# A hybrid decoder step: mixer steps placed later among the projection's products, bank copies put first

## The chip, the core and the metric

The program runs on one core of a Trainium2 chip. The metric is the device time of one launch in microseconds (us): 3565.34 us is the median of three runs before the change (3554.55 to 3570.49). A difference of 0.5%, some 18 us, is about what a measurement can tell from no change.

## The reference, cut to what matters

A trunk of two layers is run on 1024 prompt tokens and on 8 sequences of 4 new tokens each (1056 columns in all). One layer is:

```
proj = x @ w_in                                   # 46 chunks of 128 output rows
SSD : conv + SiLU, 16 heads, chunked scan, gated RMSNorm (2 groups of 8 heads)
MLA : latent queries/keys, causal attention on the prompt, paged cache for the new tokens
GDN : conv + SiLU, 4 heads, chunked delta rule (a triangular solve per chunk), gated RMSNorm
x = LayerNorm(alpha * x + [SSD | MLA | GDN] @ w_out)
```

Everything is float32. The projection's products are done as three products of rounded halves (`mm3`), the mixers' as plain float32 products.

## The kernel before, in words

Each layer has a phase one (projection and mixers) and a phase two (attention, decode over the paged cache, output projection). In phase one, `merge` (lines 422 to 444) writes TensorE's order by hand. It has two streams and a filler. Stream a runs the small per-token terms (`misc`), GDN heads 0 and 2, the latents' norm (`mla_in`) and SSD group 0. Stream b runs the input norm, GDN heads 1 and 3, the new tokens' GDN (`gdn_sample`) and SSD group 1. The filler is the projection (PSUM tiles `ps_pj`), then the latent products `mla_q` (`ps_pj<-cq`), the absorbed queries (`absorb`) and keys and values (`mla_kv`).

A stream is a generator. Where its next product needs a result of another engine it yields a number: its next step may not be placed before the planner's clock has advanced by so much. The clock counts columns of the products placed so far (`mm`, line 177: columns / 2400, times four for plain float32). While no stream is due, `merge` places filler products; when the filler is at its end or waits for something, the clock jumps to the next stream's time. So a yield does not wait: it fixes how many products stand between a step and the next one. TensorE runs them in this order and stands still where a result is late. The yield is the number that the change raises in four places:

```
        yield 2.98            # rstd, line 319: between the sums and the broadcast of 1/sqrt
        yield 5.2             # gdn_block, line 845: before the transposes of the normed output
        yield 2.03            # ssd_sample, line 1196: before each of 8 state products
```

Only TensorE's order is fixed in this way. VectorE (DVE), ScalarE (ACT), GpSimd (POOL) and SyncE's DMA queue (SP) get theirs from a scheduler that takes the program's order, readiness by its own estimate, and a priority; `high_priority()` lets what stands in it go ahead of other work that is ready. Each of these runs its queue in the order in which it was written.

Stream a's products write tiles `ps_a`, stream b's `ps_b`; each has three PSUM banks. A bank is free when the instruction that reads it out has run: a DVE or ACT copy or a DVE operation. Stream a works in `regA` (shown as `c`) and the tile `q`, stream b in `p1_b` (shown as `p_b`), their small tiles are `p_sa` and `p_sb`.

At the end of phase one these regions change hands. `absorb` writes its queries into `regA`; the attention's first query tiles are loaded into `q` (`q<-qd`, 14 DMAs); the decode's first page tiles `dec_v` lie where `p_b` and its neighbours were. The decode begins with products `ps_dS`.

Of the kernel before, what the change touches and what calls it, by code (L numbers as in the profile page):

```python
# [17 lines left out]
ALU = mybir.AluOpType  # L18
# [23 lines left out]
C_ID, C_ONES, C_BD, C_LV, C_INC, C_STR = 0, 128, 256, 384, 640, 768  # L42
C_M1, C_I1, C_L1 = 896, 928, 960
C_SUM = C_L1 + 128
C_INCS, C_STRS = C_SUM + 32, C_SUM + 64
# [82 lines left out]
class Builder:  # L128
# [48 lines left out]
    def mm(self, out, lhsT, rhs, start, stop):  # L177

        self.clock += out.free_size() * (1 if rhs.dtype in (F32R, BF16) else 4) / 2400 / {32: 4, 64: 2}.get(out.partition_size(), 1)
        return self.nc.tensor.matmul(out, lhsT=lhsT, rhs=rhs, start=start, stop=stop)  # L180
# [125 lines left out]
    def rstd(self, T, tag, ss, n, mul, eps, soon=contextlib.nullcontext):  # L306

        nc = self.nc
        ws = [(j, c, min(128, n - c)) for j, c in enumerate(range(0, n, 128))]
        ps, r = self.psum(tag), T(8)  # L310
        for j, c, w in ws:
            self.mm(ps[:w, j:j + 1], lhsT=ss[:, c:c + w], rhs=self.ones[:, 0:1], start=True, stop=True)
        full = n // 128
        with soon():
            for p, u in ((128, slice(0, full)), (n % 128, slice(full, full + 1))):
                if p:
                    nc.vector.tensor_scalar(out=r[:p, u], in0=ps[:p, u], scalar1=mul, scalar2=eps, op0=ALU.mult, op1=ALU.add)  # L317
                    nc.gpsimd.tensor_tensor(out=r[:p, u], in0=r[:p, u], in1=self.mhalf[:p, 0:1].to_broadcast([p, u.stop - u.start]), op=ALU.pow)  # L318
        yield 2.98
        ps = self.psum(tag)  # L320
        for j, c, w in ws:
            self.mm(ps[:, c:c + w], lhsT=r[:w, j:j + 1].to_broadcast([w, 128]), rhs=self.ident[:w, :w], start=True, stop=True)
        return ps[:, :n]
# [376 lines left out]
    def gdn_block(self, r, L, T, Q, h, nb, x, S, ahead):  # L700
        nc = self.nc
        k, q, v, zs, g, bt = x
        c0, _, nch = HALVES[nb]
        n = nch * 128
        cc = c0 // 128
# [7 lines left out]
        def tps(src):  # L713
            ps = self.psum(r)
            for w in ws:
                self.tp(ps[:, w], src[:, w])
            return ps[:, :n]

        def mms(lhs, rhs):
            ps = self.psum(r)  # L720
            for w in ws:
                mm(ps[:, w], lhsT=lhs[:, w], rhs=rhs[:, w], start=True, stop=True)
            return ps[:, :n]
# [7 lines left out]
        p, p2 = tps(k), tps(q)  # L731
# [8 lines left out]
        p = tps(v)  # L740
        self.tt(nc.vector, v3(vb), v3(p), bc(self.t_be[:, cc:cc + nch, h]))
        yield 3.9
        p = tps(kn)
# [4 lines left out]
        p = tps(qn)  # L748
# [13 lines left out]
        p, p2 = mms(kT, kb), mms(kT, qT)  # L762

        m = nch * 32
        Ac, Uc, Tc, Xc = (Q(m) for _ in range(4))
        c3 = lambda a: a.rearrange("p (c n) -> p c n", n=32)
        mk1 = lambda o: self.const[:, o:o + 32].unsqueeze(1).to_broadcast([128, nch, 32])
# [9 lines left out]
        def mmc(lhs, rhs):  # L777
            ps = self.psum(r)
            for c in range(nch):
                for u in gs:  # L780
                    w = slice(c * 32, c * 32 + 32)
                    mm(ps[u, w], lhsT=lhs[u, w], rhs=rhs[u, w], start=True, stop=True)
            return ps[:, :m]
# [3 lines left out]
        ahead()  # L787
        for lv in range(4):
            p = mmc(Ac, Tc)
            self.tt(nc.vector, c3(Xc), c3(p), mk1(C_L1 + 32 * lv))  # L790
            yield 1.3
            p = mmc(Uc, Xc)
            self.tt(nc.vector, Tc, Tc, p, ALU.subtract)
            nc.vector.transpose(Uc, Tc)
            yield 1.25
        v4 = lambda a: a.rearrange("p (c g n) -> p c g n", c=nch, g=4)
        for a, b, eng in ((Ti, Tc, nc.vector), (U, Uc, nc.gpsimd)):
# [3 lines left out]
        for lv in range(2):  # L801
            p = mms(at, Ti)
            self.tt(nc.vector, v3(X), v3(p), mk(C_LV + 128 * lv))
            yield 1.96
            if lv == 0:
                p = mms(U, X)
                self.tt(nc.vector, Ti, Ti, p, ALU.subtract)
                yield 1.65
                p = tps(Ti)
                nc.scalar.copy(out=U, in_=p)  # L810
            else:
                p = mms(X, U)
# [4 lines left out]
        p = mms(kbe, U)  # L817
# [4 lines left out]
        for c, w in enumerate(ws):  # L822
            p = self.psum(r)
            mm(p[:, :128], lhsT=U[:, w], rhs=vb[:, w], start=True, stop=S is None)
            if S is not None:
                mm(p[:, :128], lhsT=wT[:, w], rhs=S, start=False, stop=True)
                mm(po[:, w], lhsT=qe[:, w], rhs=S, start=True, stop=False)
            vn = Q(128)
            nc.vector.tensor_copy(out=vn, in_=p[:, :128])
            yield 1.42  # L830
            p = self.psum(r)
            mm(p[:, :128], lhsT=kd[:, w], rhs=vn, start=True, stop=True)
            mm(po[:, w], lhsT=attn[:, w], rhs=vn, start=S is None, stop=True)
            Sn = Q(128)
            if S is None:
                nc.vector.tensor_copy(out=Sn, in_=p[:, :128])
            else:
                e = (16 + h) * 16 + cc + c
                self.stt(Sn, S, self.elast[:, e:e + 1], p[:, :128], ALU.mult, ALU.add)
            S = Sn  # L840
            yield 1.3
        ro = norm(po, 1.0 / 128, RMS_EPS)
        on = t(T)
        self.tt(nc.vector, v3(on), v3(po), bc(ro))
        yield 5.2
        p = tps(on)
        self.stt(on, p, self.gnwh[:, 0:1], zs)
        self.mix_out(12 + h, c0, n, on)
# [157 lines left out]
    def ssd(self, r, g):  # L1006
        nc, l = self.nc, self.l
        R = Ring(self.reg[r][0])
        yield {-1, 17 + g * 10, 18 + g * 10}
        CT, Bt, CB, acc = R(NT), R(9 * 128), R(8 * 128 + 32), R(NT)  # L1010
        X, X2 = R.rest(), Ring(self.reg[r][1])
        BT = X(NT)
        self.dma(BT, self.pd[:, 16 + g * 2])
        self.dma(CT, self.pd[:, 17 + g * 2])
        yield 13.0
        for t0 in (0, 4, 8):
            p, p2 = self.psum(r), self.psum(r)
            for t in range(t0, min(t0 + 4, 9)):
                w = 128 if t < 8 else 32
                o = (t - t0) * 128  # L1020
                self.tp(p[:w, o:o + 128], BT[:, t * 128:t * 128 + w])
                self.mm(p2[:w, o:o + w], lhsT=BT[:, t * 128:t * 128 + w], rhs=CT[:, t * 128:t * 128 + w], start=True, stop=True)
            if t0 < 8:
                nc.scalar.copy(out=Bt[:, t0 * 128:t0 * 128 + 512], in_=p)  # L1024
                self.tt(nc.vector, CB[:, t0 * 128:t0 * 128 + 512].rearrange("p (c n) -> p c n", c=4), p2.rearrange("p (c n) -> p c n", c=4),
                        self.const[:, C_INC:C_INC + 128].unsqueeze(1).to_broadcast([128, 4, 128]))
            else:
                nc.scalar.copy(out=Bt[:32, 1024:1152], in_=p[:32, :128])
                self.tt(nc.vector, CB[:32, 1024:1056], p2[:32, :32], self.const[:32, C_INCS:C_INCS + 32])

        big = self.sm(r, F32R)
        K = slice(0, 96)
        bs = X(128)
        self.stack(bs.bitcast(F32R), Bt[0:32, 1024:1152], 1)
        self.tt(nc.gpsimd, big[K, 512:1536].rearrange("p (b n) -> p b n", b=8), bs[K].unsqueeze(1).to_broadcast([96, 8, 128]),
                self.const[K, C_BMT:C_BMT + 8].unsqueeze(2).to_broadcast([96, 8, 128]))
        for k in range(4):
            yield {19 + g * 10 + 2 * k, 20 + g * 10 + 2 * k}
            Y = Ring(X.a, X.base, X.size)
            yield from self.ssd_pair(r, Ring(Y(3 * 512)), Ring(X2.a), Ring(Y(6 * 128)), g * 4 + k, CT, Bt, CB, acc, k == 0)  # L1040
        yield from self.ssd_sample(r, X, X2, g, CT, Bt, CB, acc, big)
# [95 lines left out]
    def ssd_sample(self, r, X, T, g, CT, Bt, CB, acc, big):  # L1137
        nc, l = self.nc, self.l
# [19 lines left out]
        c3 = cm.rearrange("p (b t) -> p b t", b=8)  # L1158
# [4 lines left out]
        def old(bs):  # L1163
            for b in bs:
                q = (b % 4) * 32
                self.mm(py[q:q + 32, :], lhsT=c3[:, b], rhs=hb[b], start=b < 4, stop=b >= 4)
                el = self.elast.rearrange("p (h c) -> p h c", c=16)[:, h8, 8 + b]
                self.tt(nc.gpsimd, h3(hb[b]), h3(hb[b]), el.unsqueeze(2).to_broadcast([128, 8, 64]))
# [8 lines left out]
        p = self.psum(r)  # L1177
# [15 lines left out]
        for b in range(8):  # L1193
            if b == 4:
                old((6, 7))
            yield 2.03
            p = self.psum(r)
            self.mm(p, lhsT=b3[K, b], rhs=xs[K], start=True, stop=True)
            self.tt(nc.vector, hb[b], hb[b], p, ALU.add)
            self.dma(self.o["ssd_s"][l, :, g, b], hb[b])  # L1200
        self.tt(nc.vector, ys.rearrange("p (h n) -> p h n", n=64), py.rearrange("p (h n) -> p h n", n=64), ea.unsqueeze(2).to_broadcast([128, 8, 64]))
        yield 1.42
        p = self.psum(r)
# [779 lines left out]
```

## Time and profile before

| what | us |
|---|---|
| median of three runs | 3565.34 |
| lowest, highest | 3554.55, 3570.49 |
| profiled execution, its own time | 3572.76 |
| its span, first to last instruction | 3571.0 |
| layer 0: the attention's first score product starts at | 1060.45 |
| layer 0: the decode's first product starts at | 1075.21 |

The profile is of one execution. A row of the timeline has the start, the duration, the engine, the line, the operation, the tiles (written<-read), the shape and the count; in brackets stands how long the engine had been idle and what ended that. Plain float32 products appear twice each. Clock 1.00 is TensorE's level of 2.4 GHz, 0.50 that of 1.2 GHz; a stretch's number is the mean.

### The profile page before, as it was taken

What the parts mean: (1) busy time and instruction counts of PE and PEld (TensorE: products, weight loads), DVE (VectorE), ACT (ScalarE), POOL (GpSimd) and SP (SyncE); (2) the same over time, 40 slices, a digit from 0 to 9 for tenths busy, and PEclk for the clock granted to TensorE, in tenths of its full rate; (3) what the DMA queues carried; (4) which work ended last, traced back from release to release, by engine and by line L of the source; (5) the groups of instructions that cost most, each with busy time, mean ns of one, the idle gap of its engine ahead of it and who ended that gap; (6) DMA issues with size and microseconds to landing.
All of it is one profiled execution on the core that took longest, in us unless ns stands there. A gap on an engine that the chain in (4) does not pass through costs nothing. (4 is left out here: it accounts for less than half of the span.)

```text
span 3571.0 us, 82553 instructions
## 1 busy us (share of the span) xinstructions
PE 3124.5 (87%) x33880; PEld 2666.9 (75%) x33880; DVE 2234.9 (63%) x4646; ACT 1337.2 (37%) x3099; POOL 1124.5 (31%) x1214
## 2 busy tenths in 40 slices
PE   6889999888778988979979999898987788889797
PEld 5888988888665655559878899887886566556697
DVE  7766365687545766745586653657865466666455
ACT  5433234333133344434434332343322343434344
POOL 4434344644421211101134444355453111211000
PEclk7999999999888999989989999999998799999898
DMA  3322324555776655444424232255567755553453
GB/s 137 123 90 88 106 67 161 168 169 177 249 251 201 207 178 191 171 154 157 151 83 126 83 94 90 68 171 184 173 214 254 230 191 190 183 196 128 161 180 127
DMA packets 317070, 564.70 MB, mean 158 GB/s; under 512 B 51772, under 2 KB 218748, under 8 KB 299668
## 3 DMA queue, kind: packets, MB, share of 16 engines
q1 hardware_dynamic: 293140, 408.42, 35.9%
q0 software_dynamic: 23552, 151.01, 12.0%
q8 instruction: 266, 4.36, 0.5%
q14 instruction: 112, 0.92, 0.1%
HBM read 429.00 MB, written 130.30 MB: 157 GB/s over the span
## 5 line engine op out<-in xcount | busy, mean ns | idle before, releaser
L180 PE MATMUL ps_pj<-xh,w_r 128*128 128x384 f32 (+1 forms) x4416 | 1212.7, 342 | 50.8 <-ACT p_cv L471 17.2
L180 PEld LDWEIGHTS ps_pj<-xh,w_r 128*128 128x128 f32 x4416 | 816.1, 196 | 71.0 <-ACT p_cv L471 19.1
L180 PE MATMUL ps_pj<-xl,w_r 128*128 128x384 f32 (+1 forms) x2208 | 733.9, 332 | 4.6 <-POOL xl L153 4.0
L180 PEld LDWEIGHTS ps_pj<-xl,w_r 128*128 128x128 f32 x2208 | 432.4, 196 | 13.5 <-POOL xl L153 11.1
L180 PE MATMUL ps_m<-mix,wo 128*128 128x384 f32 (+1 forms) x2304 | 395.4, 333 | 44.1 <-DVE wo L153 19.3
L180 PEld LDWEIGHTS ps_m<-mix,wo 128*128 128x128 f32 x2304 | 385.4, 196 | 50.8 <-DVE wo L153 22.4
L156 DVE SCALAR_TENSOR_TENSOR p_cv<-p_cv,c 128x384 f32<-128x384 f32 (+1 forms) x432 | 335.0, 779 | 71.9 <-ACT p_cv L159 65.9
L180 PE MATMUL ps_dS<-dec_k,c 32*32 32x256 f32 x8192 | 314.7, 385 | 31.5 <-issue 12.8
L153 POOL TENSOR_TENSOR w_r<-w_raw,w_r 128x1024 fp32r<-128x1024 f32 (+1 forms) x98 | 233.2, 2379 | 293.5 <-ACT w_r L165 251.3
L180 PEld LDWEIGHTS ps_dS<-dec_k,c 32*32 32x32 f32 x8192 | 190.1, 106 | 135.7 <-issue 85.0
L1667 DVE STREAM_TRANSPOSE dec_k<-dec_v 128x2048 f32<-128x2048 f32 x128 | 290.9, 2282 | 0.1
L1643 POOL DMA_INDIRECT dec<-cache_k_rope,c x64 | 60.9, 951 | 566.0 <-DVE dec L1736 516.9
L153 DVE TENSOR_TENSOR wo<-c,wo 128x1024 fp32r<-128x1024 f32 x96 | 119.0, 1243 | 128.2 <-PE ps_m L180 98.3
L159 ACT ACTIVATE p_cv<-p_cv 128x384 f32<-128x384 f32 x144 | 72.8, 505 | 314.8 <-DVE p_cv L156 313.8
L1470 ACT COPY c<-ps_aT 128x512 f32<-128x512 f32 (+3 forms) x192 | 89.9, 478 | 248.0 <-PE ps_aT L150 241.2
L165 ACT CAST wo<-c 128x1024 fp32r<-128x1024 f32 x96 | 100.4, 1050 | 218.3 <-DMA c<-w_out 174.9
L1643 POOL DMA_INDIRECT dec_v<-cache_kv_latent,c x128 | 120.8, 943 | 182.9 <-PE ps_dV L180 157.6
L180 PE MATMUL ps_b<-p_b 128*128 128x128 f32 (+7 forms) x1476 | 156.8, 284 | 21.1 <-ACT p_b L1024 8.4
L1513 DVE TENSOR_REDUCE c<-ps_aS 128x1 f32<-128x512 f32 (+3 forms) x192 | 105.4, 549 | 101.7 <-PE ps_aS L180 96.3
L159 ACT ACTIVATE c<-ps_aS,c 128x512 f32<-128x512 f32 (+3 forms) x192 | 110.6, 576 | 153.7 <-DVE c L1514 138.6
L318 POOL TENSOR_TENSOR c<-c,c 128x3 f32<-128x3 f32 (+2 forms) x22 | 17.1, 783 | 472.6 <-DVE c L317 472.6
L180 PEld LDWEIGHTS ps_b<-p_b 128*128 128x128 f32 (+5 forms) x1476 | 133.6, 161 | 37.7 <-ACT p_b L1024 9.9
(325 smaller groups left out, 5601.6 us busy)
## 6 DMA issues: line engine op xcount, KB each, us to landing
c<-w_out SPq DMA_DIRECT2D x96, 512.0 KB
w_raw<-w_in SPq DMA_DIRECT2D x92, 512.0 KB
pd<-p_cv SPq DMA_DIRECT2D x164, 192.0 KB
p_b<-pd SPq DMA_DIRECT2D x66, 256.0 KB
c<-pd SPq DMA_DIRECT2D x64, 256.0 KB
q<-rowd SPq DMA_DIRECT2D x48, 256.0 KB
p_b<-rowd SPq DMA_DIRECT2D x48, 256.0 KB
pd<-p_cv SPq DMA_DIRECT2D x82, 144.0 KB
```

The costliest lines, as they stand in the source:

```text
L153: eng.tensor_tensor(out=out, in0=a, in1=b, op=op)
L156: self.nc.vector.scalar_tensor_tensor(out=out, in0=a, scalar=s, in1=b, op0=op0, op1=op1)
L159: self.nc.scalar.activation(out=out, in_=in_, func=func, **kw)
L165: self.nc.scalar.copy(out=hi, in_=src)
L180: return self.nc.tensor.matmul(out, lhsT=lhsT, rhs=rhs, start=start, stop=stop)
L318: nc.gpsimd.tensor_tensor(out=r[:p, u], in0=r[:p, u], in1=self.mhalf[:p, 0:1].to_broadcast([p, u.stop - u.start]), op=ALU.pow)
L1470: nc.scalar.copy(out=t[:, :w], in_=p[:, :w])
L1513: nc.vector.reduce_max(out=m, in_=ps[:, :w], axis=AX.X)
L1643: nc.gpsimd.indirect_dma_start(out=out, out_offset=None, in_=src, in_offset=bass.IndirectOffsetOnAxis(ap=idx[:, c:c + 1], axis=0))
L1667: nc.vector.transpose(T[r].rearrange("p j s k -> p j (s k)"), V[:, :, r * 128:r * 128 + 128])
```

## The change

Four yields are raised or added, all in phase one, and the instructions that read a mixer's bank out are put under `high_priority()` at three places.

```diff
@@ rstd
-        yield 2.98
+        yield 5.5
@@ gdn_block, the four levels of the 32-row solve, and the scan over chunks
             p = mmc(Ac, Tc)
-            self.tt(nc.vector, c3(Xc), c3(p), mk1(C_L1 + 32 * lv))
+            with self.tc.high_priority():
+                self.tt(nc.vector, c3(Xc), c3(p), mk1(C_L1 + 32 * lv))
             yield 1.3
             p = mmc(Uc, Xc)
-            self.tt(nc.vector, Tc, Tc, p, ALU.subtract)
-            nc.vector.transpose(Uc, Tc)
+            with self.tc.high_priority():
+                self.tt(nc.vector, Tc, Tc, p, ALU.subtract)
+                nc.vector.transpose(Uc, Tc)
...
-            nc.vector.tensor_copy(out=vn, in_=p[:, :128])
+            with self.tc.high_priority():
+                nc.vector.tensor_copy(out=vn, in_=p[:, :128])
...
-            if S is None:
-                nc.vector.tensor_copy(out=Sn, in_=p[:, :128])
-            else: ...
+            with self.tc.high_priority():
+                if S is None:
+                    nc.vector.tensor_copy(out=Sn, in_=p[:, :128])
+                else: ...
@@ gdn_block, before the transposes of the normed output
-        yield 5.2
+        yield 7.5
@@ ssd, the start of a group
         for t0 in (0, 4, 8):
+            if t0:
+                yield 2.5
             p, p2 = self.psum(r), self.psum(r)
...
-            if t0 < 8:
-                nc.scalar.copy(out=Bt[:, t0 * 128:t0 * 128 + 512], in_=p)
-                self.tt(nc.vector, CB[...], p2..., ...)
-            else: ...
+            with self.tc.high_priority():
+                if t0 < 8:
+                    nc.scalar.copy(out=Bt[:, t0 * 128:t0 * 128 + 512], in_=p)
+                    self.tt(nc.vector, CB[...], p2..., ...)
+                else: ...
@@ ssd_sample
         for b in range(8):
-            yield 2.03
+            yield 2.03 if b else 7.0
```

What this does to the order of the instructions is seen at three places of layer 0 (layer 1 is alike).

TensorE at the start of SSD group 0 (stream a). `ps_a<-c_58,c_144` is a transpose of the B rows, `ps_a<-c_144` the product of B with C. Before, the second set of four follows the first at once:

```order
L150 MATMUL ps_a<-c_58,c_144 128x128
L180 MATMUL ps_a<-c_144 128x128
L150 MATMUL ps_a<-c_58,c_144 128x128
L180 MATMUL ps_a<-c_144 128x128
L150 MATMUL ps_a<-c_58,c_144 128x128
L180 MATMUL ps_a<-c_144 128x128
L150 MATMUL ps_a<-c_58,c_144 128x128
L180 MATMUL ps_a<-c_144 128x128
```

After, from the last pair of the first set to the first pair of the second:

```order
L180 MATMUL ps_b<-p_sb 128x512
L180 MATMUL ps_pj<-xh,w_r 128x384
L180 MATMUL ps_pj<-xl,w_r 128x384
L180 MATMUL ps_pj<-xh,w_r 128x384 x2
L180 MATMUL ps_pj<-xl,w_r 128x384
L180 MATMUL ps_pj<-xh,w_r 128x384 x2
L180 MATMUL ps_pj<-xl,w_r 128x384
L180 MATMUL ps_pj<-xh,w_r 128x384
L150 MATMUL ps_a<-c_58,c_144 128x128
L180 MATMUL ps_a<-c_144 128x128
```

Fifteen products of the projection (six of them ahead of the first row shown) and one of stream b now stand between the two sets.

SyncE's DMA queue at the end of phase one. `c_144<-qd` are the loads of `absorb` (c_144 is `regA`), `q<-qd` those of the attention's first queries. Before, the last of the 14 query loads and what follows:

```order
L136 DMA q<-qd_161 64x4x128
L136 DMA q<-qd_162 64x2x128
L136 DMA q<-qd_161 32x4x128 x2
L136 DMA q<-qd_162 32x4x128
L136 DMA c_144<-w_ukT 64x2048
L136 DMA c_144<-qd_161 64x8x32
L136 DMA c_144<-qd_161 32x8x32
L136 DMA c_144<-qd_162 64x8x32
L136 DMA c_144<-qd_162 32x8x32
L136 DMA mixd<-p_b 128x288 x4
```

After, the loads of `absorb` come right behind the last stores of the queries, and the 14 loads stand further down:

```order
L136 DMA qd_161<-stage 128x384
L136 DMA qd_162<-stage 128x384
L136 DMA kr<-krx 64x1024
L136 DMA kr<-krx 32x1024
L136 DMA c_144<-w_ukT 64x2048
L136 DMA c_144<-qd_161 64x8x32
L136 DMA c_144<-qd_161 32x8x32
L136 DMA c_144<-qd_162 64x8x32
L136 DMA c_144<-qd_162 32x8x32
L136 DMA p_b<-ssd_st 128x512 x2
L136 DMA yd<-q 128x4x32
```

The 14 loads now stand behind stream a's last load into the tile `q` and its last stores from it.

TensorE at the change from phase one to phase two. `w_r,ck` are the value products of `mla_kv`, `ps_aS` the attention's scores. Before:

```order
L180 MATMUL ps_pj<-w_r,ck 128x512 x6
L180 MATMUL ps_a<-w_r,ck 128x512 x6
L180 MATMUL ps_aS<-kT,q 128x256 x2
L180 MATMUL ps_aS<-kr,q 128x256
L180 LDWEIGHTS c_124
L180 MATMUL ps_aS<-c_124 128x128
```

After, to the first three of the six small products of the norm that stand just before the same scores:

```order
L180 MATMUL ps_a<-w_r,ck 128x512 x6
L180 MATMUL ps_b<-p_sb 128x512 x2
L180 MATMUL ps_b<-c_58,p_b 128x32
L180 MATMUL ps_b<-p_b 64x32 x2
L180 MATMUL ps_b<-c_58,p_b 128x32
L180 MATMUL ps_b<-p_b 64x32 x2
L180 MATMUL ps_b<-c_58,p_b 128x32
L180 MATMUL ps_b<-p_b 64x32 x2
L180 MATMUL ps_b<-c_58,p_b 128x32
L180 MATMUL ps_b<-p_b 64x32 x2
L180 MATMUL ps_b<-c_58,p_b 128x1 x2
L180 MATMUL ps_b<-c_58,p_b 32x1
```

The last steps of stream b, the end of the new tokens' SSD and its norm, now stand behind the filler's last product, with nothing between them.

## Rows read from the trace of the kernel before

**Rows 1.** Busy time by stretch: PE, PEld, DVE, ACT, POOL; PEclk; DMA share, GB/s.
```profile
100.00:960.00 860.00, 779.82 (x7145) 731.27 (x7144) 551.44 (x1154) 297.90 (x728) 395.33 (x432) 0.96 0.43 137
```
**Rows 2.** Waits of PE, 60 to 1070 us: total, times, longest.
```profile
PE ps_pj L180 <- ACT p_cv L471: 9.3, 3, 3.8
PE ps_a L180 <- ACT c L1024: 9.2, 1, 9.2
...
PE ps_a L180 <- DVE p_sa L153: 7.4, 5, 4.8
...
PE ps_b L180 <- DVE p_sb L153: 5.2, 6, 2.1
PE ps_pj L180 <- DVE stage L153: 4.9, 4, 1.5
...
PE ps_a L180 <- DVE p_sa L829: 4.3, 3, 3.3
PE ps_b L180 <- ACT p_b L1024: 4.2, 1, 4.2
PE ps_a L180 <- DVE p_sa L836: 4.0, 1, 4.0
...
PE ps_a L180 <- POOL c L318: 2.4, 1, 2.4
```
**Rows 3.** Waits of PE in layer 1, 1830 to 2860 us.
```profile
PE ps_a L180 <- ACT c L1024: 9.5, 1, 9.5
PE ps_a L180 <- DVE c L153: 9.5, 1, 9.5
```
**Rows 4.** Timeline of all engines at the start of SSD group 0.
```profile
665.09 6.47 DVE L1092 TENSOR_SCALAR q<-q,c 128x128 f32<-128x128 f32 x7 [4.16 <-DMA q<-rowd]
...
673.57 0.79 PE L180 MATMUL ps_a<-c 128*128 128x128 f32 x2 [9.17 <-ACT c L1024]
```
**Rows 5.** Timeline of PE at the first state product of stream a.
```profile
920.48 0.42 PE L180 MATMUL ps_pj<-xh,w_r 128*128 128x384 f32 x1
...
922.49 0.34 PE L180 MATMUL ps_pj<-xh,w_r 128*128 128x384 f32 x1
927.62 0.77 PE L180 MATMUL ps_a<-p_sa 96*128 96x512 f32 x1 [4.79 <-DVE p_sa L153]
```
**Rows 6.** Busy time by stretch, around that wait and around the wait of `absorb`.
```profile
922.00:933.00 11.00, 6.21 (x23) 5.78 (x22) 7.07 (x14) 3.61 (x6) 4.24 (x4) 0.69 0.59 204
1031.00:1053.00 22.00, 13.14 (x48) 11.81 (x49) 4.88 (x9) 3.56 (x7) 2.55 (x3) 0.61 0.71 207
```
**Rows 7.** Timeline of PE, end of phase one.
```profile
1013.85 0.30 PE L180 MATMUL ps_b<-c,p_b 128*128 128x32 f32 x2
...
1024.23 0.94 PE L180 MATMUL ps_b<-c,p_b 128*128 128x128 f32 x6
...
1039.86 7.00 PE L180 MATMUL ps_a<-c 64*128 64x32 f32 x32 [8.93 <-DVE c L153]
...
1060.45 0.40 PE L180 MATMUL ps_aS<-kT,q 128*128 128x256 f32 x2
...
1075.21 1.10 PE L180 MATMUL ps_dS<-dec,c 32*32 32x256 f32 x16 [1.21 <-DVE dec L1722]
```
**Rows 8.** Timeline of SyncE's DMA queue, end of phase one.
```profile
1020.32 0.45 SPq L136 DMA_DIRECT2D yd<-p_b  x1
...
1024.09 0.38 SPq L136 DMA_DIRECT2D p_b<-yd  x1
...
1025.06 8.34 SPq L136 DMA_DIRECT2D q<-qd  x14
...
1036.69 2.01 SPq L136 DMA_DIRECT2D mixd<-p_b  x4
```
**Rows 9.** Timeline of POOL: the decode's first page load.
```profile
1041.69 1.22 POOL L1643 DMA_INDIRECT dec_v<-cache_kv_latent,c  x1 [1.42 <-DMA c<-gated]
```
**Rows 10.** Timeline of DVE in the first GDN blocks.
```profile
219.81 0.69 DVE L153 TENSOR_TENSOR p_b<-ps_b,p_sb 128x512 f32<-128x512 f32 x1 [2.18 <-POOL p_sb L674]
```

More of the change, by code (lines that the diff above doesn't have):

```diff
@@ L834, in gdn_block @@
             Sn = Q(128)
-            if S is None:
-                nc.vector.tensor_copy(out=Sn, in_=p[:, :128])
-            else:
-                e = (16 + h) * 16 + cc + c
-                self.stt(Sn, S, self.elast[:, e:e + 1], p[:, :128], ALU.mult, ALU.add)
+            with self.tc.high_priority():
+                if S is None:
+                    nc.vector.tensor_copy(out=Sn, in_=p[:, :128])
+                else:
+                    e = (16 + h) * 16 + cc + c
+                    self.stt(Sn, S, self.elast[:, e:e + 1], p[:, :128], ALU.mult, ALU.add)
             S = Sn
@@ L1022, in ssd @@
                 self.mm(p2[:w, o:o + w], lhsT=BT[:, t * 128:t * 128 + w], rhs=CT[:, t * 128:t * 128 + w], start=True, stop=True)
-            if t0 < 8:
-                nc.scalar.copy(out=Bt[:, t0 * 128:t0 * 128 + 512], in_=p)
[L1025 to L1029, printed above, removed]
+            with self.tc.high_priority():
+                if t0 < 8:
+                    nc.scalar.copy(out=Bt[:, t0 * 128:t0 * 128 + 512], in_=p)
+                    self.tt(nc.vector, CB[:, t0 * 128:t0 * 128 + 512].rearrange("p (c n) -> p c n", c=4), p2.rearrange("p (c n) -> p c n", c=4),
+                            self.const[:, C_INC:C_INC + 128].unsqueeze(1).to_broadcast([128, 4, 128]))
+                else:
+                    nc.scalar.copy(out=Bt[:32, 1024:1152], in_=p[:32, :128])
+                    self.tt(nc.vector, CB[:32, 1024:1056], p2[:32, :32], self.const[:32, C_INCS:C_INCS + 32])
         big = self.sm(r, F32R)
```

## The prediction

> **What bounds the kernel now.** I read the busy time by stretch first. In phase one of layer 0 TensorE is busy 779.8 of 860 us (91%) and VectorE 551.4 (64%) [rows 1]: TensorE's fixed order sets the time, and the change can give at most its idle tenth and what the clock loses. Second come the waits by cause [rows 2]. The ones that this change touches are the ACT copies of line 1024 in both streams (9.2 and 4.2 us), the DVE results on p_sa and p_sb (7.4, 5.2, 4.3 and 4.0), the GpSimd power of the norms on line 318 (2.4), and, at one place, an addition of `absorb` (8.93, seen in the timeline of the end [rows 7]). Layer 1 has the two longest again, 9.5 and 9.5 [rows 3], so I work out one layer and double it. Third is the timeline at each of them, for what stands behind the wait, and fourth the end of phase one on TensorE, SyncE's queue and GpSimd [rows 7 to 9], because the new order leaves work there.
>
> **The change part by part, one layer.** The sum is made against the profiled execution, 3572.8 us; that is 7.4 above the median of 3565.3.
>
> A filler product at the full clock takes 0.17 us: twelve of them lie between 920.48 and the end of the last at about 922.5 plus 0.34 [rows 5]. A unit of the planner's clock is about 6.25 products of 384 columns, so 1.06 us; 2.5 units are 2.7 us.
>
> SSD group 0: the second set of four needs a bank that an ACT copy frees, and waits 9.17 us. The copy is not late by its place alone: in ACT's order it stands behind exponentials of `q`, which need DVE's line 1092, and DVE itself stood 4.16 us for the load `q<-rowd` and then took 6.47 us for seven of eight [rows 4]. In the new order two exponentials of `q` still stand ahead of the copy, so the priority changes nothing here; only the 15 filler products put between the sets do, 15 x 0.17 = 2.6 us. Bounds: 0 (the load comes later too) and 9.2; I take 2.6. SSD group 1: 4.2 us of wait, the same spacing, 2.7; bounds 0 and 4.2.
>
> First state product of `ssd_sample` in stream a: 4.79 us of wait for a DVE operation [rows 5]; the yield grows by 5 units, 5.3 us, so it goes: 4.8. In stream b there is no such wait, and the 5 units only move it later. `rstd`: 2.5 units more, 2.7 us, against 2.4 us of wait: 2.4. Bounds of both: 0 and their size. The raised yield before the GDN transposes removes no wait that the rows show; at nothing its cover is the filler, which lasts until the end of the stream, and where it ends is priced below.
>
> GDN under priority: p_sa and p_sb waits are 7.4 + 5.2 + 4.3 + 4.0 = 20.9, less the 4.8 already counted, 16.1 us. DVE's order in the first blocks, where the 4.0 of line 836 is, does not change at all, since three convolution operations still stand ahead of that copy. Further on the copies do move forward. I take 4; bounds 12 (all the others) and -4 (below).
>
> `absorb`: its 8.93 us are SyncE's. Its loads of `qd` stand behind 14 query loads that take 8.34 us to issue [rows 8]; in the new order they come first, and between the last latent product and `absorb` there is more work of the mixers. The wait goes: 8.9; bounds 4 and 8.9. The 14 loads come later, but the scores that need them also stand behind the steps of stream b: issued within 9 us of `absorb`, against 14 us of value products, so nothing.
>
> The clock. In 1031 to 1053 it was granted at 0.61, so 17 of 22 us were at 1.2 GHz, and from 1039.86 on TensorE had work: 12 us at half speed lose 6. Around the 4.79 us wait it was 0.69: some 5 us of work, 2.5 lost [rows 6]. With the shorter waits this is 10 or so; the new idle time at the end takes some back. I take 8; bounds 0 and 12.
>
> Sum of the gains: 2.6 + 2.7 + 4.8 + 2.4 + 4 + 8.9 + 8 = 33.4 us.
>
> The end of phase one. Today stream b is over before the filler: its last broadcast is at 1024.23, and the first scores follow the last value product at 1060.45 with nothing between, the decode's first product 14.8 us later [rows 7]. In the new order two state products, twelve small ones and the norm stand bare behind the last value product; call its end E. From 1013.85 to 1025.2 the same steps took 11.3 us with some 7 us of filler in them [rows 7]; bare, I count 10 us to the scores, 6 of them idle. The second part is the pages. The first page load came 3.0 us after the last of four stores `mixd<-p_b` was issued [rows 8, 9]: it overwrites what stream b's norm has to store first. That norm stores `yd`, and its load of it was issued 3.8 us later [rows 8]. So: E + 6 for the store, + 3.8, + 4 for load and products, + 2 for the stores, + 3: page load at E + 19. It moves 2 MB for the first unit; I allow 7 us and put the first decode product at E + 26 instead of E + 14.8: -11. Bounds: -10 (pages hidden behind the scores, which alone reach E + 25) and -37 (as long as the page waited for its use today, 1041.69 to 1075.21, 33.5 us [rows 7, 9]); the near one, since today's distance was set by the order and not by the load.
>
> Latent products: `ps_pj` waits 4.9 us for DVE in that stretch [rows 2], and more SSD blocks now fall into it: -3, bounds 0 and -10.
>
> Net per layer 33.4 - 14 = 19.4; two layers 39. 3572.8 - 39 = 3534 for a profiled run, 3526 against the median.
>
> **A rule that speaks against the change.** DVE stood idle for 2.18 us at 219.81 before an operation of stream b whose GpSimd result was late, while convolution operations stood behind it in its queue [rows 10]. The Trainium skill, "Perfetto Trace Analysis", section "Tensor Engine Instruction (MATMUL, LD_WEIGHTS)", says that ACT, DVE and GpSimd are strict FIFO, and the row agrees. By that rule a copy put ahead of ready work stops the queue until its product has run; this is the second rival below.
>
> **Rivals.** First, more than forecast. The whole 9.2 and 4.2 of the SSD starts and 12 of GDN go: 8.1 + 8 = 16 more per layer, 3494. For it: once the streams sit later, everything that they wait for has had longer. Against it: DVE's wait for `q<-rowd` [rows 4] is tied to the same stream and moves with it.
>
> Second, no change by the queues. Copies that stand first in DVE wait for products that run later than the scheduler thought; convolutions fall behind, and the projection waits for its banks instead. It already waits 9.3 us for ACT line 471 [rows 2]. If GDN turns to -4, the conv waits double (-9) and the latents cost 10, a layer nets 33.4 - 8 - 9 - 11 - 10 = -5 to +5: 3565. Against it: DVE is 64% busy [rows 1].
>
> Third, slower, by the end of phase one. If the first page load is really late and long, the decode starts at E + 45 to E + 52 and the layer pays 30 to 37 instead of 11, and the gain in the middle without `absorb` and its clock is only about 19. It decides from 30 us on: 33.4 - 3 - 37 = -7 per layer, with the clock term gone -15: 3580 to 3595. For it: the page load waits for a chain of three DMAs [rows 8, 9]. Against it: two thirds of the 33.5 us today passed in other work.
>
> That the change does not do what it says is part of the forecast: the priority does nothing in the first GDN blocks and at SSD group 0.
>
> **Chances.** Forecast (3495 to 3547) 0.50; more (under 3495) 0.17; no change 0.20; slower 0.13. So faster by over 0.5% (under 3547, the bound of what a measurement can tell, 18 us) 0.67, within it 0.20, slower 0.13. The range 3480 to 3578 leaves out a third of the first rival and most of the third.
>
> **What would show it.** Right: no wait over 1 us at the first state product and at line 318; the wait for the Bt copy 6 to 7 us; `absorb` without a wait and the clock at 1.00 through the value products; a hole of about 6 us in three pieces after the last value product, and the first decode product some 26 us behind it. Wrong: `ps_pj` waits on p_cv well over today's, or a decode that starts over 40 us after the last value product, or the SSD waits gone whole.

## The result, and the profile after

The changed kernel takes 3590.38 us (median of 5 runs, 3579.86 to 3595.48) against 3565.34 of the kernel before: a ratio of 1.0063, 95% interval 1.0043 to 1.0083. I had forecast 3526, so the sign was wrong. The profiled execution has a span of 3593.7 us, 22.7 more than before: 9.1 of them in layer 0, 13.6 in layer 1.

First the stretches of [rows 1] and [rows 6] again, with the same columns.

```profile
100.00:960.00 860.00, 774.14 (x7065) 729.65 (x7064) 529.88 (x1117) 295.11 (x725) 385.38 (x423) 0.95 0.42 134
1031.00:1053.00 22.00, 22.00 (x90) 18.11 (x91) 5.14 (x9) 4.99 (x10) 5.07 (x13) 0.77 0.42 124
```

From `absorb` on TensorE has no idle time left and the granted clock rose from 0.61 to 0.77, two fifths of the way to the 1.00 that I had forecast. In the long middle stretch nothing was won: 80 products fewer ran in the same 860 us, at a clock of 0.95 where it was 0.96. The waits of TensorE from 60 to 1060 us (total, times, longest) say why.

```profile
PE ps_pj L180 <- DVE p_cv L156: 11.2, 5, 5.4
PE ps_pj L180 <- ACT p_cv L471: 9.3, 3, 3.8
...
PE ps_b L180 <- DVE p_b L153: 8.9, 5, 3.9
PE ps_pj L180 <- DVE stage L153: 7.9, 3, 5.5
...
PE ps_b L150 <- POOL p_b L153: 4.3, 1, 4.3
...
PE ps_a L180 <- DVE p_sa L840: 4.0, 1, 4.0
...
PE ps_a L180 <- DVE p_sa L153: 3.5, 4, 1.2
...
PE ps_b L180 <- ACT p_b L1031: 1.8, 2, 1.4
```

Of the waits that [rows 2] leads with, that for line 471 is as it was, and that for stream a's copy of line 1024 is gone; the other copies' waits are smaller, but for that of line 836 (840 now). Others grew, four of them by 17.7 us in sum: for the convolutions (p_cv, VectorE), for stream b's operations on p_b (on VectorE and on GpSimd), and for the latents' stage (4.9 in [rows 2]). In the kernel before, the first three of these were (60 to 1070 us):

```profile
PE ps_pj L180 <- DVE p_cv L156: 7.3, 5, 4.9
...
PE ps_b L180 <- DVE p_b L153: 2.0, 2, 1.5
...
PE ps_b L150 <- POOL p_b L153: 0.4, 1, 0.4
```

VectorE's row loads at the start of SSD group 0 stand first, for [rows 4]; the end of phase one follows, on TensorE (with that start ahead of it), then SyncE's queue, VectorE and GpSimd; it answers to [rows 7 to 9]. A row without a bracket had no idle time before it that counts.

```profile
716.64 0.87 DVE L1099 TENSOR_SCALAR q<-q,c 128x128 f32<-128x128 f32 x4 [1.22 <-DMA q<-rowd]
```
```profile
718.17 0.49 PE L180 MATMUL ps_a<-c 128*128 128x128 f32 x2 [1.40 <-DVE c L153]
...
1030.92 1.45 PE L180 MATMUL ps_a<-c 64*128 64x32 f32 x6 [3.40 <-issue]
...
1051.28 1.56 PE L180 MATMUL ps_a<-w_r,ck 128*128 128x512 f32 x6
...
1057.40 0.22 PE L180 MATMUL ps_b<-c,p_b 128*32 128x1 f32 x2 [1.46 <-DVE p_b L1225]
1058.71 1.78 PE L180 MATMUL ps_b<-c,p_b 128*128 128x128 f32 x6 [1.09 <-POOL p_b L318]
1060.43 0.80 PE L180 MATMUL ps_aS<-kT,q 128*128 128x256 f32 x2
...
1069.84 0.77 PE L180 MATMUL ps_aS<-kT,q 128*128 128x256 f32 x2 [8.28 <-DVE p_b L156]
...
1086.73 1.10 PE L180 MATMUL ps_dS<-dec,c 32*32 32x256 f32 x16 [2.11 <-DVE dec L1729]
```
```profile
1060.40 0.60 SPq L136 DMA_DIRECT2D yd<-p_b  x1
...
1063.63 0.47 SPq L136 DMA_DIRECT2D p_b<-yd  x1
...
1068.45 1.79 SPq L136 DMA_DIRECT2D mixd<-p_b  x4
```
```profile
1067.91 1.79 DVE L156 SCALAR_TENSOR_TENSOR p_b<-p_b,c,ps_b 128x288 f32<-128x288 f32 x4 [10.04 <-issue]
...
1085.58 0.29 DVE L1520 TENSOR_REDUCE c<-ps_aS 128x1 f32<-128x128 f32 x1 [1.72 <-PE ps_aS L180]
...
1085.97 0.70 DVE L1729 STREAM_TRANSPOSE dec<-dec 128x512 f32<-128x512 f32 x1
```
```profile
1072.75 1.22 POOL L1650 DMA_INDIRECT dec_v<-cache_kv_latent,c  x1 [13.57 <-DMA dec<-qxd]
```

The last value product ends at some 1052.8; before it ended where the first score began [rows 7]. So it is 8 us earlier. But the first score is at the same 1060.4, and the decode's first product 11.5 us later.

Where these 11.5 us lie can be read off. In both kernels eight scores stand in TensorE's order ahead of the decode's first product. In the kernel before the second of them followed the first at once:

```profile
1060.84 0.48 PE L180 MATMUL ps_aS<-kT,q 128*128 128x256 f32 x2
```

In the changed kernel it waited 8.28 us (10.18 in layer 1), because VectorE reads the first score out behind stream b's norm, and the norm began at 1067.91 only, 4.3 us after its load of `yd` was issued. (The row names no releaser; in e10 and e12 the same row names this load, 4.1 and 3.9 us after its issue.) From the second score to the decode it took 16.9 us instead of 14.4; the granted clock from 1060 to 1090 was 0.50. For its pages the decode did not wait: VectorE's first transpose for it (line 1729) follows the attention's last read of a score without idle time.

### The profile page after: what moved, and what is told of

Read it like the earlier page. It is cut to its first block, busy times and chain, and to the rows that moved or that the text cites. A ratio compares the mean times of both kernels' runs of the same rounds, so it can differ in the third digit from the quotient of the medians.

```text
span 3593.7 us, 82518 instructions
## 1 busy us (share of the span) xinstructions
PE 3137.9 (87%) x33880; PEld 2669.3 (74%) x33880; DVE 2233.8 (62%) x4646; ACT 1331.5 (37%) x3099; POOL 1124.6 (31%) x1214
## 5 line engine op out<-in xcount | busy, mean ns | idle before, releaser
L156 DVE SCALAR_TENSOR_TENSOR p_cv<-p_cv,c 128x384 f32<-128x384 f32 (+1 forms) x432 | 344.5, 800 | 87.7 <-ACT p_cv L159 81.1
L1537 ACT ACTIVATE c<-c 128x512 f32<-128x512 f32 (+3 forms) x192 | 111.2, 612 | 105.0 <-DVE c L1535 51.4
```

Of the source, the lines that this page charges most:

```text
L156: self.nc.vector.scalar_tensor_tensor(out=out, in0=a, scalar=s, in1=b, op0=op0, op1=op1)
L1537: nc.scalar.mul(out=Pm[:, o:o + w], in_=Pm[:, o:o + w], mul=r[:, b:b + 1])
```

## The experiments

The kernels of a block ran on one chip, beside the kernel before, whose median was 3506, 3571, 3569, 3507 and 3580 us in the five blocks; ratios are against that. "Pj to score" is the time from the layer's first projection product to its first score, "score to dS" from there to the decode's first product, "score to m" to the first product of the output projection, each read from the timeline of the run's profile, layer 0 / layer 1. Compare "score to m" within a block only: it differs by some 35 us between blocks (e9 and e15, e13 and e17). The profiles of the kernel before and of e9, which are the same kernel, differ by up to 6 us in a cell, so smaller differences say nothing.

| block, kernel | ratio (95%) | pj to score | score to dS | score to m |
|---|---|---|---|---|
| before | 1 | 1028 / 1011 | 15 / 16 | 518 / 522 |
| changed | 1.0063 (1.0043 to 1.0083) | 1028 / 1004 | 26 / 28 | 528 / 543 |
| 1: e1 priority alone | 0.9954 (0.9932 to 0.9975) | 1026 / 1009 | 11 / 13 | 484 / 479 |
| 1: e2 four yields alone | 1.0089 (1.0066 to 1.0112) | 1035 / 1017 | 24 / 27 | 504 / 499 |
| 1: e3 yields 2.5 and 7.0 | 0.9950 (0.9930 to 0.9970) | 1013 / 996 | 28 / 28 | 496 / 494 |
| 1: e4 yields 5.5 and 7.5 | 1.0135 (1.0114 to 1.0155) | 1040 / 1027 | 21 / 22 | 500 / 494 |
| 2: e5 priority, 2.5, 7.0 | 0.9940 (0.9920 to 0.9959) | 1005 / 991 | 29 / 28 | 530 / 528 |
| 2: e6 yield 5.5 alone | 1.0009 (0.9992 to 1.0027) | 1016 / 1013 | 29 / 29 | 529 / 526 |
| 2: e7 yield 7.5 alone | 1.0138 (1.0113 to 1.0162) | 1043 / 1023 | 23 / 27 | 531 / 540 |
| 2: e8 changed, b's tail early | 1.0108 (1.0084 to 1.0132) | 1027 / 1006 | 39 / 39 | 538 / 537 |
| 3: e9 before, again | 1.0014 (1.0001 to 1.0027) | 1032 / 1016 | 15 / 15 | 520 / 516 |
| 3: e10 changed, 5.2 for 7.5 | 0.9991 (0.9976 to 1.0005) | 1013 / 994 | 25 / 25 | 531 / 529 |
| 3: e11 7.5 in stream a | 1.0066 (1.0048 to 1.0083) | 1037 / 1031 | 15 / 15 | 528 / 516 |
| 3: e12 7.5 in stream b | 1.0087 (1.0065 to 1.0109) | 1030 / 1010 | 23 / 25 | 534 / 530 |
| 4: e13 b's tail late | 1.0048 (1.0031 to 1.0066) | 1031 / 1006 | 32 / 31 | 498 / 490 |
| 4: e14 stream a alone | 0.9888 (0.9867 to 0.9909) | 1017 / 995 | 11 / 11 | 481 / 482 |
| 4: e15 4.0 for 5.2 | 0.9975 (0.9959 to 0.9991) | 1030 / 1010 | 11 / 13 | 487 / 482 |
| 4: e16 e14 with 4.0 | 0.9927 (0.9906 to 0.9948) | 1010 / 1008 | 14 / 13 | 486 / 475 |
| 5: e17 e13, gate first | 1.0042 (1.0028 to 1.0056) | 1035 / 1013 | 22 / 23 | 532 / 528 |
| 5: e18 e5, gate first | 0.9932 (0.9919 to 0.9945) | 1007 / 994 | 23 / 24 | 530 / 529 |

**Block 1: the parts.** My first theory was that the longer yields push stream b behind the projection, and that the bare tail is the loss. The rival was priority.

```diff
 e1 (against changed): all four yields at their old values
 e2 (against before):  all four yields raised, no high_priority()
 e3 (against before):
+            if t0:
+                yield 2.5
...
-            yield 2.03
+            yield 2.03 if b else 7.0
 e4 (against before):
-        yield 2.98
+        yield 5.5
...
-        yield 5.2
+        yield 7.5
```


> The kernel before with only the three pieces under priority; all four yields as before. Theory (the longer yields push stream b past the end of the filler, and the loss is there): the first scores at 1060 +-3 and the decode's first product some 15 us behind them as before, no wait of 8 us before the score on q; total 3545 to 3572, ratio 0.995 to 1.002. Rival (priority makes the queues worse: copies that stand first hold up DVE's convolutions): new waits of ps_pj for p_cv, total 3580 to 3595, ratio 1.004 to 1.008.

> The kernel before with the four yields raised and no priority. Theory (yields push stream b out): the tail of stream b behind the last value product and the 8 us wait before the score on q stay, the decode's first product 25 to 30 us behind the first score; total 3580 to 3600, ratio 1.004 to 1.010. Rival (queues under priority): 3535 to 3565, ratio 0.992 to 1.000, since the yields alone remove waits.

> The kernel before with two of the four yields: 2.5 between the sets of SSD's start, 7.0 before the first state product. They add 5.0 + 5.0 units to each stream, about half of what stream b was pushed. Theory: most of the removed waits (9.2, 4.2, 4.8 us per layer) go here; stream b ends near the filler's end, with less of a tail; total 3545 to 3570, ratio 0.994 to 1.001. Rival (any later step is paid for by a new wait elsewhere, one for one): 3562 to 3575, ratio 0.999 to 1.003.

> The kernel before with the other two yields: 5.5 in the norms, 7.5 before the GDN transposes. These are taken 8 to 14 times per stream, so they push stream b by the larger part, and remove only some 2.4 us of wait per layer. Theory: a bare tail behind the last value product and a late decode; total 3570 to 3590, ratio 1.001 to 1.007. Rival (queues): 3560 to 3570, ratio 0.998 to 1.001.

Priority gains, so the rival on queues falls; where it gains is not shown, since this block has no profile of the kernel before. The two yields that remove a wait gain; the two that stand where there is hardly one lose 1.35%. The e3 kernel already shows a second thing: its first score comes 15 us earlier per layer, and the decode's first product hardly at all.

**Block 2: which of the two, and is it the tail?**

```diff
 e5 (against changed): 2.98 and 5.2 put back
 e6 (against before):
-        yield 2.98
+        yield 5.5
 e7 (against before):
-        yield 5.2
+        yield 7.5
 e8 (against changed; stream b, SSD group 1 only):
-        yield 5.5
+        yield 1.5
...
-            yield 2.03 if b else 7.0
+            yield 0.3 if b else 1.0
```


> The changed kernel with two yields put back to their old values (2.98 in the norms, 5.2 before the GDN transposes); priority and the two other yields stay. If the two parts that gained alone (0.9954 and 0.995) act at different waits, they multiply: ratio 0.990 (0.986 to 0.993). Rival: both remove the same waits, and together they give what one gives: 0.994 to 0.997.

> The kernel before with 5.5 in the norms alone. The two long yields together gave 1.0135. Theory (the loss is the end of phase one: stream b's last norm comes late, its region is free late, pages and decode come late): this yield stands in every norm of both SSD groups, stream b's last one too, so it carries most of it, 1.006 to 1.012. Rival (loss in the middle, where GDN steps of the two streams fall together): 0.998 to 1.003.

> The kernel before with 7.5 before the GDN transposes alone. Theory (end of phase one): it moves everything behind it later as well, by 6 x 2.3 units, and stream b then ends 6 filler products before the end: 1.003 to 1.008, with pages 10 us or more later. Rival (loss in the middle): 1.008 to 1.013, with new waits of ps_b and of ps_pj on p_cv between 470 and 700 us, and the first score later by 8 us or more.

> The changed kernel, but in stream b alone the state products of the new tokens are placed 0.3 units apart (1.0 before the first) and the norm's yield of SSD group 1 is 1.5. TensorE's order is that of the changed kernel word for word until some 14 us behind the first latent product; then stream b ends 54 filler products before the end and not behind it. Theory (of the loss, the end of phase one is the larger part: 8 us of bare steps, 8 us of wait for the late norm, pages later): ratio to the kernel before 0.995 to 1.001 where the changed kernel has 1.006, the decode's first product 15 us or so behind the first score. Rival (loss in the middle): 1.004 to 1.008.

The whole loss of the pair is the 7.5 before the GDN transposes. It costs in both parts of the layer: against e9 (the kernel before, in the next block, whose time is within 0.1% of this block's) pj to score is 11 and 7 us longer, score to m 11 and 24. The 5.5 in the norms is not without effect, though: in e6 the first score comes 16 and 4 us earlier than in e9, and the 14 us more from there to the decode take it back. Against my theory, e8, with no bare tail, became slower still: 39 us from the first score to the decode. In its trace the attention stood for a load of its gate:

```profile
1086.21 0.29 DVE L156 SCALAR_TENSOR_TENSOR c<-ps_aO,c 128x128 f32<-128x128 f32 x1 [21.36 <-DMA c<-gated]
```

The first score came no earlier than in the changed kernel (1027 / 1006 against 1028 / 1004), so the bare products were not the price. Nor did stream b's early end on TensorE free its regions early: its norm ran on VectorE at 1049.91, 10 us ahead of the first score, where in the kernel before it ran 27 us ahead. The parts of e5 don't multiply (0.994, not 0.990): its first score comes some 20 us earlier than that of e1, and it pays at score to dS.

**Block 3: undo the one number, and split it by stream.**

```diff
 e10 (against changed):
-        yield 7.5
+        yield 5.2
 e11, e12 (against before):
-        yield 5.2
+        yield 7.5 if r == "a" else 5.2        # e12: "b"
```


> The kernel before itself, for a profile from the same chip as the next three: ratio 1.000 (0.998 to 1.002); from the first score to the output projection 518 to 522 us per layer if that stretch is the same on this chip, or some 480 as on the chip of the first four.

> The changed kernel with one number put back: 5.2 before the GDN transposes. If this yield alone turned the gain into a loss (it cost 1.38% alone), the rest is worth what its parts were: ratio 0.991 to 0.996. Rival (the parts don't add, stream b still ends bare behind the last value product): 0.999 to 1.004.

> The kernel before with 7.5 before the GDN transposes of stream a alone (four blocks, 9.2 units). Theory by length (each stream pays for how much later it ends; stream b's end is what phase two waits for): little, 1.000 to 1.005, pages as early as before. Rival (the two streams' steps fall onto each other): as much as both together, 1.008 or more, or a gain; not between.

> The kernel before with 7.5 before the GDN transposes of stream b alone. Theory by length: most of the 1.38%, 1.008 to 1.014; the first page 20 us or more later against the first score than in the control, and the first score itself later by 5 us or more per layer. Rival (coincidence): 0.996 to 1.004.

The control is within 0.14% of itself; its interval leaves out 1, so a difference of this size says nothing. With one number put back the loss is gone (0.9991), but not turned into the gain that I expected. The cost of 7.5 adds up over the streams (0.66% and 0.87% against 1.38%), so length and not a coincidence of both. But the places differ: stream a's delay costs 5 and 14 us before the first score (against e9), 8 and 1 behind it, and nothing at the decode's start; stream b's delay costs nothing before the first score, and 14 us per layer behind it. For e11 the waits of TensorE that grew most against e9 are these, the first of e9, the others of e11 (e9's for p_b are not among its thirteen longest, so at most 3.5):

```profile
PE ps_pj L180 <- DVE p_cv L156: 6.8, 3, 3.9
```
```profile
PE ps_pj L180 <- DVE p_cv L156: 10.1, 7, 2.4
...
PE ps_b L180 <- POOL p_b L153: 6.0, 3, 5.3
PE ps_b L180 <- DVE p_b L153: 5.7, 2, 3.9
```

**Block 4: stream b's end by itself, and the use of it.**

```diff
 e13 (against before; TensorE's order is the same up to the first latent product):
-            yield 2.03
+            yield 14.0 if r == "b" and not b else 2.03
 e14 (against changed):
-        yield 7.5
+        yield 5.2
     the other three longer yields only for r == "a"; stream b has 2.98, none, 2.03
 e15 (against before), e16 (against e14):
-        yield 5.2
+        yield 4.0
```


> The kernel before with one number: 14.0 units in place of 2.03 before stream b's first state product. TensorE's order is that of the kernel before until the first latent product; then stream b ends 24 filler products before the last value product and not 72. Theory (phase two's start is paid by stream b's end alone): first score within 5 us of the control's place in its layer, from there to the output projection 10 to 15 us longer per layer, ratio 1.005 to 1.009. Rival (the later end comes with other moves, and itself costs little): 0.998 to 1.003.

> The changed kernel with 5.2 before the GDN transposes and the three other longer yields in stream a alone; stream b has its old ones and ends 72 filler products before the end, as in the kernel before. Theory (stream b's end costs at phase two's start, the waits that go are mostly stream a's): first score 12 to 20 us earlier per layer and phase two's start as before, ratio 0.988 to 0.993, faster than every run so far. Rival (phase two's start is dearer for another reason): 0.994 to 0.998.

> The kernel before with 4.0 in place of 5.2 before the GDN transposes in both streams (four blocks each, 4.8 units earlier). Theory (cost by length, 1.38% for 9.2 units, and linear): 0.993 to 0.997. Rival (coincidence at 7.5, or new waits before the transposes because the norm isn't done): 0.999 to 1.006.

> As stream a alone, with 4.0 before the GDN transposes in both streams. If the last two each gain, they multiply: 0.984 to 0.990. Rival: 4.0 stands too early, the transposes wait for the norm, and it is no better than stream a alone.

Stream b's end alone costs 0.48%, 17 us or 8 per layer, with the first score no later than it was. Its TensorE, queue, VectorE and GpSimd rows:

```profile
1062.51 0.40 PE L180 MATMUL ps_aS<-kT,q 128*128 128x256 f32 x2
...
1092.34 0.47 PE L150 MATMUL ps_aT<-c,c 128*128 128x128 f32 x1 [21.58 <-ACT c L1530]
...
1094.82 1.11 PE L180 MATMUL ps_dS<-dec,c 32*32 32x256 f32 x16 [1.24 <-DVE dec L1722]
```
```profile
1068.31 6.03 SPq L136 DMA_DIRECT2D q<-qd  x7
...
1087.47 0.91 SPq L136 DMA_DIRECT2D c<-gated  x2
```
```profile
1091.49 0.29 DVE L156 SCALAR_TENSOR_TENSOR c<-ps_aO,c 128x128 f32<-128x128 f32 x1 [21.32 <-DMA c<-gated]
```
```profile
1061.94 1.22 POOL L1643 DMA_INDIRECT dec_v<-cache_kv_latent,c  x1 [11.07 <-ACT V L1370]
```

In e14 stream b ends as early as before; the first gate load and the first page go out 22 and 19 us ahead of the first score, and the decode follows it by 11 us:

```profile
1027.33 0.45 SPq L136 DMA_DIRECT2D c<-gated  x1
```
```profile
1030.06 1.21 POOL L1650 DMA_INDIRECT dec_v<-cache_kv_latent,c  x1 [1.28 <-DMA mixd<-p_b]
```
```profile
1049.28 0.40 PE L180 MATMUL ps_aS<-kT,q 128*128 128x256 f32 x2
...
1060.55 1.10 PE L180 MATMUL ps_dS<-dec,c 32*32 32x256 f32 x16 [1.24 <-DVE dec L1729]
```

At 3466.3 us against 3507.4 it beats the kernel before, and by the ratios the changed one too. Against e10 it differs only in stream b's yields, and these are worth 1.0% by the two ratios, which are of two blocks. A yield of 4.0 gains 0.25%, little more than the control's 0.14% and a third of what the cost of 7.5 would give in proportion, and it adds nothing to e14 (0.9927 in e16 beside 0.9888), so 5.2 stands near its best place.

**Block 5: is it the gate load's place in the queue?**

```diff
 e17 (against e13), e18 (against e5):
+                    with self.tc.high_priority():
+                        self.dma(gt, self.gated[:, pr, i * 128:i * 128 + 128])
-                    self.dma(gt, self.gated[:, pr, i * 128:i * 128 + 128])
```


> As the kernel with stream b's tail late (14.0 units before its first state product; 1.0048), and the attention's loads of its gate under priority, which puts the first two ahead of the decode's loads in SyncE's queue; the page loads stay as late. Theory (the place in the queue is the price): no wait of DVE over 5 us for a gate load, from the first score to the decode's first product 11 to 18 us instead of 31 to 32, ratio 0.998 to 1.002. Rival (the pages' burst is the price): the wait only changes its name, 27 to 32 us as before, ratio 1.004 to 1.006.

> The same for the kernel with priority and the two shorter yields (0.994, where DVE waits 13.7 us for the gate): theory 0.987 to 0.991, from the first score to the decode's first product 15 to 19 us instead of 28; rival 0.993 to 0.996.

The wait for the gate is gone and another has its place: in e17 VectorE's first transpose for the decode, and with it the decode's first product, waits for its own pages.

```profile
1073.25 0.34 SPq L136 DMA_DIRECT2D c<-gated  x1
1073.63 1.40 SPq L136 DMA_DIRECT2D mixd<-p_b  x3
```
```profile
1079.11 1.21 POOL L1644 DMA_INDIRECT dec_v<-cache_kv_latent,c  x1 [22.97 <-ACT c L159]
```
```profile
1089.58 0.71 DVE L1723 STREAM_TRANSPOSE dec<-dec 128x512 f32<-128x512 f32 x1 [11.54 <-DMA dec<-cache_k_rope,c]
```

Score to dS fell from 32 to 22 us, and yet the ratio is 1.0042, the interval overlapping that of e13. It is the same in e18: 23 and 24 us where e5 had 29 and 28, a wait of 12.99 us for the same transpose, and 0.9932 beside 0.9940. By their ratios both came out as the rival said. The runs aren't a clean answer: in e17 the gate's load stands ahead of the stores `mixd<-p_b`, for which the first page waits in the row of e14, and the first page went out 11 us behind the first score, where in e13 it was 0.6 ahead of it. What is shown is that stream b's late end costs; which of the loads behind it comes last depends on the queue's order.

## Why the prediction was wrong

**The step that failed first: the yield before the GDN transposes.** "The raised yield ... removes no wait that the rows show; at nothing its cover is the filler." Alone it costs 1.38%. I looked for what it removes, found nothing, and took "nothing stands in it" for "it costs nothing". It makes every later step of its stream 9.2 units later per layer; in stream a this brings new waits (e11) and in stream b a later end (e12). Of the 64 us between forecast and result, putting this one number back returns 0.72% (e10), some 26 us.

**The second: the end of phase one, -11, measured -19 and -20, and not for the pages.** Most of the chain was right. Counted from the last value product's end E (1052.8): first score E + 8 (forecast E + 10; its bare steps left 2.5 us idle, not 6), load of `yd` E + 11 (E + 10), first page E + 20 (E + 19). From there I let the decode wait for its pages, to E + 26. It came at E + 34, and the pages had landed by then. What I had put into the chain to the pages, stream b's norm and its load of `yd`, I had left out of the chain to the scores ("pages hidden behind the scores, which alone reach E + 25"): VectorE reads the scores behind that norm, the second score came at E + 17, and the rest of the attention's steps made it E + 34. The 7 us that I allowed for the page load are not tested in this kernel; in e17, where VectorE did wait for it, there were 10.5 from the first page's issue to the transpose (1079.11 to 1089.58). I had also taken the near bound of a term whose far one was -37. And I had the tail's idle time as the price; in e10, where the tail is nearly covered, score to m is 11 and 13 us longer than in e9 all the same. What is paid is the wait for a load that follows stream b's late end: that of `yd` for its own norm in the changed kernel, in e10 and in e12 (the second score waits 8.28, 5.98 and 5.76 us), the gate's in e8 and e13, the pages in e17.

**The gains: 33.4, less 3 for the latents.** The last value product should have been 30 us earlier and was 8 and 15. The named waits of layer 0 gave 25.4 us in sum, which is what I had forecast for them; that the sum agrees is luck. SSD group 0 went from 9.17 to 1.40, a gain of 7.8 for 2.6 (VectorE waited only 1.22 us for the row load, not 4.16 as in [rows 4], so that load did not come later with the stream); `absorb` from 8.93 to 3.40, 5.5 for 8.9; the waits on p_sa and p_sb, without that of the state product, gave 2.5 for 4, with that of line 836 unchanged at 4.0 as said; the first state product and line 318 in stream a have no wait left, as forecast. The four waits named under the result took 17.7 us of it back, and smaller ones moved both ways; I had counted new waits at -3, in the latents alone. The clock gave nothing. Up to the first score TensorE runs the same products (kernel before, changed, e9, e10):

```profile
32.00:1060.45 1028.45, 908.02 (x7754) 839.51 (x7755) 657.16 (x1333) 367.23 (x868) 463.14 (x504) 0.94 0.46 145
```
```profile
32.00:1060.43 1028.43, 913.08 (x7755) 846.26 (x7755) 652.96 (x1329) 365.35 (x869) 461.01 (x502) 0.93 0.44 141
```
```profile
32.00:1064.11 1032.11, 909.13 (x7754) 843.48 (x7755) 657.16 (x1333) 367.05 (x868) 462.89 (x504) 0.94 0.46 145
```
```profile
32.00:1045.33 1013.33, 897.53 (x7754) 832.43 (x7754) 661.89 (x1328) 366.40 (x868) 459.12 (x502) 0.95 0.45 144
```

In the changed kernel they took 5 us more, and the idle time fell by 5 us only. In layer 1 their time was the same (894.0 and 894.3) and the idle time fell by 7. So the term of 8 us for the clock came out at -5 and 0. In e10, with 5.2 put back, it is there: 11.6 and 6.3 us less busy time than in e9. Its last value product is 19 and 23 us earlier than in e9, so some 11 and 8 us of the missing gain are the 7.5, in layer 0 by the clock and not by idle time (115.4 and 115.8 us idle in the changed kernel and in e10).

**The other points.** The rule on strict queues, my second rival, does not decide: priority alone is 0.9954. The third rival had the right sign and the right place, the end of phase one, but the wrong cause and condition: it asked for late pages and for E + 45 with all the gains intact, while E + 34 was enough with the gains at a half or less. "The 14 loads come later ... so nothing" held: no score waits for them. Layer 1 loses a further 9 us between the decode's first product and the output projection. Seven of these lie in the last stretch (kernel before, then changed): the same products took 28.05 us at a clock of 0.62 where they took 20.74 at 0.78, with 15 us idle in both. I did not find what lowered the clock. Nor is it shown which of stream a's new waits follows from which step of GDN.

```profile
3302.00:3338.00 36.00, 20.74 (x139) 10.79 (x138) 11.37 (x50) 10.94 (x22) 0.00 (x0) 0.78 0.37 118
```
```profile
3318.00:3361.00 43.00, 28.05 (x138) 12.50 (x135) 11.04 (x48) 10.47 (x21) 0.00 (x0) 0.62 0.30 94
```

## What to carry to other kernels

A gap written into an order by hand is not free because other work fills it: everything behind it in the same chain comes later, and a large part of the price is at the chain's end, where regions are handed on and the next stage's loads begin. So give room only where a row shows a wait, to the stream that is not the last to release anything, and price the end by the first load that it holds back, in every queue where something stands behind that load. When a wait vanishes and the time stays, look for the next thing that waits in the same queue.

## What was not expected of the hardware

A small load can be late because it is issued late. The slices below are of 1 us each, from 1060 on, in e13. From 1065 to 1086 the DMA engines are 80% busy or more at some 240 to 420 GB/s. In this time SyncE's queue stood 9.4 us, in three pieces, until query loads that it had issued itself had landed (first row), and so the two gate loads of 64 KB each were issued 25 us after the first page. Once issued, they took some 4 us (1087.47 to 1091.49). Whether the page loads or the queue's own loads made the landings late, no run separates.

```profile
SPq L136 <- DMA q<-qd: 9.4, 3, 4.6
```
```profile
DMA  2004799899999999999999899943987123437860
GB/s 90 0 0 66 197 401 418 328 401 283 311 381 412 416 421 418 410 362 374 406 378 397 349 326 239 236 109 56 168 309 226 30 66 78 99 75 165 285 167 1
```

That DMAs from SyncE's and GpSimd's queues run on the same 16 engines and interleave is what the Trainium skill says ("Trainium Kernel Development and Optimization", section "Key Constraints"); the trace agrees: from 1060 to 1100 GpSimd's queue took 49.1% and SyncE's 24.8% of the 16 engines' time.
